# First loads in an order of their own, and the first two output tiles together, in a hybrid pooling and SSD decoder step

## The chip, the cores and the metric

The kernel runs on one core of one Trainium2 chip. The metric is device time in microseconds (us) for one execution, the median of several runs. The core has a matrix engine (TensorE, PE in the profile, with its weight loads as PEld), a vector engine (VectorE, DVE), a scalar engine (ScalarE, ACT), a general engine (GpSimd, POOL) and a sync engine (SyncE, SP) that issues nearly all the transfers. Each engine takes its instructions in one fixed order. The order of the compiled program is made beforehand by a scheduler that simulates the program, so an instruction can stand far from where the source has it.

## The reference, cut to what matters

One decoder layer works on 1024 prompt tokens and 64 sample tokens with model width 1024. All data are 32-bit floats.

```python
def swiglu(x, w_in, w_out):
    gu = x @ w_in
    g, u = gu[..., :D_FF], gu[..., D_FF:]
    return (jax.nn.silu(g) * u) @ w_out          # D_FF = 2816

def layer(x, ...):
    x = x + 0.5 * swiglu(rmsnorm(x, norm_ffn1[l]), ffn1_w_in[l], ffn1_w_out[l])
    mix, ... = token_mixing(rmsnorm(x, norm_mix[l]), ...)
    x = x + mix
    x = x + 0.5 * swiglu(rmsnorm(x, norm_ffn2[l]), ffn2_w_in[l], ffn2_w_out[l])
    return x, ...
# then one final rmsnorm
```

The token mixing (pooling branch and state-space branch with gates) is not touched by the change.

## The kernel before, in words

**Halves and splits.** The tokens are cut in two halves: half 0 has 512 columns, half 1 has 512 prompt and 64 sample columns, 576 in all, computed as two pieces of 288. Activations lie with the channel on the 128 partitions. For accuracy each operand is the sum of a high and a low part; a product of two operands is three matmuls (high by high, high by low, low by high). `load_w` loads 4 blocks of 128x128 weights (256 KB) into a `wraw` buffer (6 of them), ACT copies out the high part `wh` (L264) and DVE the low part `wl` (L265; 3 buffers each).

**Start.** `load_x` (L605 on) loads a half of x token by token in tiles of 128x512 (`xin`, L618; eight for half 0, ten for half 1), squares them on ACT (L627), finds the reciprocal root on DVE, makes diagonal matrices `dg` (L637, on DVE and POOL in turn) and multiplies by them on PE, which transposes and scales at once (`ptx`, and `pxs` for the samples). ACT, DVE and POOL then make `xn`, `hi` and `lo`. In the source the first weights come first, then x of half 0, then more weights; x of half 1 is a chain of its own. `load_consts` loads 13 small constants; `Dcol` is read from `d_skip` at every second element (L234).

**First product of an FFN.** There are 22 tiles of 128 channels (`NFF`). The first three (`N_PLAIN`) are computed directly, for half 0 and then half 1 (`ffn_in_plain`, banks `pg` and `pu`). The others use a seven-product scheme (`ffn_in`, `wino`, banks `pw`), whose operands are made from x beforehand (`combine`, much of it on POOL). The weights of a tile are combined and split for it (L405 on POOL, L411 on ACT, L412 on DVE). All but the last three tiles (`N_APART`) serve both halves with one set of weights; the last three are computed for half 0 and then, with the weights loaded again, for half 1. An `ffn_in` tile is evacuated by ACT (L504, L512) and DVE (L516 to L521), and the result `g` is stored to DRAM (`hd`, L523).

**Second product.** For each half the 22 stored tiles are loaded (`hr`, L578) and split into `hh` (ACT, L302) and `hr` (DVE, L304). Their buffers come from the `act` pool (58 buffers), of which the operands of the first product hold 56; a few come from the `fx` pool (17). Then the eight output tiles are computed one after the other over all 22 blocks (`po`), each with six weight loads, and added to x (L588). In the second FFN, `half` begins the transposes of the final output after four tiles.

**Order.** `pe` counts the PE work written so far, and side chains (`start`, `tick`) come in when it reaches their due time. `after1` starts the norm for the mixing of half 0 (`norm_split`, pace `HN_PACE`), which is needed after half 1's second product. `dma` is always SP's queue.

Of the kernel before, what the change touches and what calls it, by code (L numbers as in the profile page):

```python
# [14 lines left out]
P = 128  # L15
D = 1024
KD = D // P
# [18 lines left out]
N_ACT, N_BIG, N_PD = 58, 3, 4  # L36
N_RAW, N_W = 6, 3
N_FX, N_S, N_PDF = 17, 4, 6
N_PLAIN, N_APART = 3, 3

PRODUCTS = (("1", 0), ("2", 1), ("6", 0), ("5", 2), ("7", 0), ("3", 2), ("4", 0))

# [3 lines left out]
STEP_S = 2.5  # L46
GP = (0.7, 1.2)
PACE = 2.0
HN_PACE = 0.5
MP = 2.0  # L50
R_WAIT0 = 3.0
R_WAIT = 5.0
# [9 lines left out]
def tile_hybrid_pool_ssd_macaron(  # L62
# [23 lines left out]
    def act(shape=(P, 576), dt=F32, name="a"):  # L86
        return sp.tile(list(shape), dt, tag="act", bufs=N_ACT, name=nm(name))
# [17 lines left out]
    def fx(dt=F32, name="x"):  # L105
        if stage["name"] == "mix":
            return act((P, 576), dt, name)
        return stage["p"].tile([P, 576], dt, tag="fx", bufs=N_FX, name=nm(name))
# [111 lines left out]
    Dcol = cp.tile([P, 16], F32, tag="Dcol", name="Dcol")  # L220
    rd_n = [0]
    hp = [0]

    def load_consts():

        yield from load_cols(nr0, nr1)
        yield from load_cols(nr1, nr)
        for t, src in ((tri, c_tri), (strict, c_strict), (tri_s, c_tri_s), (strict_s, c_strict_s), (bsel, c_bsel),
                       (invcnt, c_invcnt.partition_broadcast(P)), (dtb, dt_bias[0].rearrange("(h o) -> h o", o=1)),
                       (Abc, a_log[0].partition_broadcast(P))):  # L230
            dma(t, src)
        dsk = d_skip[0].rearrange("(q h) -> h q", h=2)
        for hh in range(2):
            dma(Dcol[hh * HD : (hh + 1) * HD, :], dsk[hh].partition_broadcast(HD))  # L234
        for i in range(3):
            dma(bsel3[i * 32 : (i + 1) * 32, :], c_bsel[0:32, 0:4])
        yield 12
        for j in range(4):
            V.tensor_scalar_mul(cwh[:, j, :], cols[:, i_cw[j] : i_cw[j] + 24], 0.5)
        V.tensor_scalar_mul(cwh[:, 4, :], cols[:, i_cb : i_cb + 24], 0.5)  # L240
        S.activation(Abc, Abc, AF.Exp)
        V.tensor_scalar_mul(Abc, Abc, -1.0)
# [9 lines left out]

    ahead = {}

    def load_w(w, k0, nk, c0, ncol=P):

        if (k0, c0) in ahead:
            return ahead.pop((k0, c0))
        raw, wh, wl = (sp.tile([P, 4 * P], d, tag=t, bufs=n, name=nm(t))[:, : nk * ncol]
                       for t, d, n in (("wraw", F32, N_RAW), ("wh", F32R, N_W), ("wl", F32R, N_W)))  # L260
        dma(raw.rearrange("p (k c) -> p k c", c=ncol),
            w[k0 * P : (k0 + nk) * P, c0 : c0 + ncol].rearrange("(k p) c -> p k c", p=P))
        with tc.high_priority(hp[0]):
            S.activation(wh, raw, AF.Copy)  # L264
            V.tensor_tensor(wl, raw, wh.bitcast(F32), op=ALU.subtract)  # L265
        return wh.rearrange("p (k c) -> p k c", c=ncol), wl.rearrange("p (k c) -> p k c", c=ncol)
# [12 lines left out]
    def dense(w, rk0, nk, c0, xs, tag="pd", name="pd"):  # L279

        out = banks(xs, tag, name)
        for kb in range(0, nk, 4):
            n4 = min(4, nk - kb)
            wh, wl = load_w(w, rk0 + kb, n4, c0)
            for kk in range(n4):
                products(out, wh, wl, kk, slice(0, P), xs, kb + kk, nk)
                tick()
        return out
# [254 lines left out]
    def ffn(wi, wo, prep, after, half=None):  # L543

        X, todo, behind = [{}, {}], [], []
        for h in HALVES:
            finish(prep[h][0])
            x = prep[h][1][0]  # L550
            gen = combine(h, x[3], x[1], x[2], X[h], T_PACE)

            def first(gen):
                for p in gen:
                    if p is None:
                        return
                    yield p

            c = start(first(gen), T_AT)
            for ff in range(N_PLAIN):  # L560
                ffn_in_plain(wi, ff, x[:3])
            todo.append(c)
            behind.append(start(rest(c, gen)))
        for c in behind:
            finish(c)
        for ff in range(N_PLAIN, NFF - N_APART):
            ffn_in(wi, ff, [(h, X[h]) for h in HALVES])
        for h in HALVES:
            for ff in range(NFF - N_APART, NFF):
                ffn_in(wi, ff, [(h, X[h])])  # L570
        for h in HALVES:
            N = NTOK[h]
            parts = [], []
            for k in range(NFF):
                slot = (lambda d, n_: act((P, 576), d, n_)) if half or k < NFF - 2 else fx
                t, a = slot(F32, "hr"), slot(F32R, "hh")
                t = t[:, :N]
                dma(t, hdram[h][k])  # L578
                split(t, a[:, :N], t.bitcast(F32R))
                parts[0].append(a)  # L580
                parts[1].append(t.bitcast(F32R))
            xt = []
            for m in range(KD):
                x_ = fx(name="x")
                dma(x_[:, :N], xspill[h][m])
                po = dense(wo, 0, NFF, m * P, [(h, *parts)], name="po")[0]
                for pt, (a, b) in zip(po, PIECES[h]):
                    V.scalar_tensor_tensor(x_[:, a:b], pt[:, : b - a], 0.5, x_[:, a:b], op0=ALU.mult, op1=ALU.add)  # L588
                xt.append(x_)
                if half and m == KD // 2 - 1:  # L590
                    half(h, xt)
            after(h, xt)

# [13 lines left out]
    def load_x(h, out):  # L607
# [2 lines left out]
        N = NTOK[h]  # L610
        blocks = blocks_of(h)
        nb = len(blocks)
        raws = []
        for src, _, c in blocks:
            raws.append([])
            for q in range(2):
                t = act((P, 512), name="xin")
                dma(t[:c, :], src[:, q * 512 : (q + 1) * 512])  # L618
                raws[-1].append(t)
        yield X1_AT if h else 0.2  # L620
        ss = small((P, 4, 5), "xss", 2)
        if h == 1:
            G.memset(ss, 1.0)
        for i, (_, c0, c) in enumerate(blocks):
            for q in range(2):
                junk = act((P, 512), name="junk")
# [7 lines left out]
        dg = act((P, 576), name="dg")  # L634
        dg = [dg[:, i * P : i * P + b[2]] for i, b in enumerate(blocks)]
        for i, (_, c0, c) in enumerate(blocks):
            (V if i % 2 else G).tensor_scalar_mul(dg[i][:c, :c], ident[:c, :c], ss[:c, 2, i : i + 1])  # L637
        if h == 1:
            pq = psum("ps", "pxs")
            for k in range(KD):  # L640
# [57 lines left out]

    def after1(h, xt):
        if h == 0:  # L700
            ch["hn"] = start(norm_split([t[:, : NTOK[0]] for t in xt], 0, i_gm, hn, HN_PACE))
        for m in range(KD):
            dma(xspill[h][m], xt[m][:, : NTOK[h]])

    st = open_stage("ffn1", N_PDF)
    finish(start(load_cols(0, nr0)))
    prep1 = []
    for kb in (0, 4):
        for c0 in (0, FF):
            ahead[kb, c0] = load_w(wi1, kb, 4, c0)  # L710
        if kb == 0:
            for h in HALVES:
                o = []
                prep1.append((start(load_x(h, o)), o))
                if h == 0:
                    prep1[0][0].step()

    def turn():
        for h in HALVES:
# [759 lines left out]
```

## Time and profile before

| | us |
|---|---|
| median of 3 runs | 3026.63 (3025.07 to 3032.89) |
| the profiled execution's own time | 3030.0 |
| its span in the trace | 3028.2 |
| PE busy | 2928.0 |
| DVE busy | 1779.1 |
| ACT busy | 1279.1 |
| POOL busy | 438.1 |

Times in the rows are from the span's start. A row of the timeline has the start, the length, the engine, the line and the operation, output and input, the count, and in brackets the idle time of the engine before it with what ended it. `SPq` rows are issues of transfers, not the transfers themselves. In a row of stretches each engine's busy time stands with its number of instructions, then the granted PE clock (1.00 is full speed), the share of time in which the 16 DMA engines were busy, and GB/s. A busy PE is not PE at its peak, because matmuls overlap; the count of matmuls in a stretch tells its pace. In rows of waits the numbers are the total, the times and, in PE's waits, the longest.

### The profile page before, as it was taken

To read this page: it belongs to the slowest core of one execution; us is meant where nothing else is said; L and a number is where in the kernel's file an instruction comes from. 1 tells how busy PE (TensorE), PEld (TensorE's weight loads), DVE (VectorE), ACT (ScalarE), POOL (GpSimd) and SP (SyncE) were. 2 spreads that over 40 slices of the span, in tenths; PEclk is the share of its full clock that TensorE was granted. 3 is DMA by queue.
4 is the path that set the end of the run, shared out by engine and by line. 5 is a ranking of instruction groups with operands and counts; after the bars stand their busy time and mean duration, and the time that the engine had idled before them with its cause. 6 is when DMAs were issued, how large, how long until landed. Compare 5 with 4: busy or idle time off the path is not lost. (4 is left out here: it accounts for less than half of the span.)

```text
span 3028.2 us, 51543 instructions
## 1 busy us (share of the span) xinstructions
PE 2928.0 (97%) x19636; PEld 2714.0 (90%) x19636; DVE 1779.1 (59%) x3479; ACT 1279.1 (42%) x2580; POOL 438.1 (14%) x497
## 2 busy tenths in 40 slices
PE   6999999999999999999999999999999999999998
PEld 5999999789988878787999989999989999997898
DVE  4644347534273898777725986977775343374442
ACT  4443335423243665434424654543443333353332
POOL 3433335000000000000000110100023333350000
PEclk9999999999999999999999999999999999999999
DMA  4442224753334333445333334344443222245542
GB/s 128 132 134 92 79 83 124 225 157 119 101 96 124 113 106 96 112 121 175 97 104 103 107 112 132 93 130 133 152 133 102 72 79 75 77 144 154 170 146 72
DMA packets 527722, 356.29 MB, mean 118 GB/s; under 512 B 27418, under 2 KB 468880, under 8 KB 527466
## 3 DMA queue, kind: packets, MB, share of 16 engines
q1 hardware_dynamic: 527458, 352.99, 39.0%
q8 instruction: 154, 2.52, 0.4%
q14 instruction: 94, 0.77, 0.1%
q10 hardware_dynamic: 16, 0.00, 0.0%
HBM read 295.85 MB, written 57.29 MB: 117 GB/s over the span
## 5 line engine op out<-in xcount | busy, mean ns | idle before, releaser
L264 ACT ACTIVATE wh<-wraw 128x512 fp32r<-128x512 f32 x636 | 392.2, 619 | 853.0 <-PE po L160 287.0
L265 DVE TENSOR_TENSOR wl<-wraw,wh 128x512 fp32r<-128x512 f32 x636 | 437.4, 690 | 510.5 <-ACT wh L264 492.0
L160 PE MATMUL pw<-hi,wh 128*128 128x288 f32 (+1 forms) x1216 | 352.3, 290 | 6.4 <-DVE t L516 6.4
L160 PE MATMUL pw<-X,wh 128*128 128x256 f32 (+1 forms) x1824 | 349.7, 290 | 8.6 <-ACT t L512 7.2
L160 PE MATMUL pw<-hi,wl 128*128 128x288 f32 (+1 forms) x1216 | 351.1, 289 | 0.5 <-DVE wl L412 0.5
L160 PE MATMUL pw<-lo,wh 128*128 128x288 f32 (+1 forms) x1216 | 350.8, 289 | 0.0
L160 PEld LDWEIGHTS pw<-X,wh 128*128 128x128 f32 x1824 | 288.6, 190 | 11.1 <-ACT t L512 8.6
L160 PE MATMUL po<-hh,wh 128*128 128x288 f32 (+1 forms) x1056 | 290.8, 331 | 7.6 <-ACT hh L302 5.6
L160 PE MATMUL po<-hr,wh 128*128 128x288 f32 (+1 forms) x1056 | 290.1, 330 | 1.0 <-DVE hr L304 1.0
L160 PE MATMUL po<-hh,wl 128*128 128x288 f32 (+1 forms) x1056 | 289.4, 329 | 0.5 <-DVE wl L265 0.4
L160 PE MATMUL pw<-X,wl 128*128 128x256 f32 (+1 forms) x912 | 263.6, 289 | 0.0
L160 PEld LDWEIGHTS pw<-hi,wh 128*128 128x128 f32 x1216 | 230.6, 190 | 7.8 <-DVE t L516 7.8
L160 PEld LDWEIGHTS pw<-hi,wl 128*128 128x128 f32 x1216 | 230.4, 189 | 0.8 <-DVE wl L412 0.7
L160 PEld LDWEIGHTS pw<-lo,wh 128*128 128x128 f32 x1216 | 230.5, 190 | 0.0
L412 DVE TENSOR_TENSOR wl<-s,wh 128x512 fp32r<-128x512 f32 x176 | 129.5, 740 | 160.1 <-ACT wh L411 156.6
L160 PEld LDWEIGHTS po<-hh,wh 128*128 128x128 f32 x1056 | 180.4, 190 | 25.4 <-ACT hh L302 8.6
L160 PEld LDWEIGHTS po<-hr,wh 128*128 128x128 f32 x1056 | 180.9, 190 | 17.0 <-DVE hr L304 3.6
L160 PEld LDWEIGHTS po<-hh,wl 128*128 128x128 f32 x1056 | 180.7, 190 | 14.9 <-DVE wl L265 1.4
L411 ACT ACTIVATE wh<-s 128x512 fp32r<-128x512 f32 x176 | 110.6, 630 | 168.0 <-PE pw L160 164.6
L160 PEld LDWEIGHTS pw<-X,wl 128*128 128x128 f32 x912 | 174.0, 191 | 0.0
L160 PE MATMUL pc<-hi,wh 128*128 128x288 f32 (+1 forms) x576 | 162.1, 335 | 0.4 <-ACT craw L750 0.3
L160 PE MATMUL pc<-hi,wl 128*128 128x288 f32 (+1 forms) x576 | 159.4, 329 | 0.0
(334 smaller groups left out, 6454.3 us busy)
## 6 DMA issues: line engine op xcount, KB each, us to landing
wraw<-in_w_in_dram SPq DMA_DIRECT2D x260, 256.0 KB
wraw<-in_ffn_w_in_dram SPq DMA_DIRECT2D x224, 256.0 KB
wraw<-in_ffn_w_out_dram SPq DMA_DIRECT2D x160, 256.0 KB
ab<-acsd SPq DMA_DIRECT2D x64, 256.0 KB
wraw<-in_ssd_w_out_dram SPq DMA_DIRECT2D x64, 256.0 KB
hd<-g SPq DMA_DIRECT2D x44, 288.0 KB
hr<-hd SPq DMA_DIRECT2D x44, 288.0 KB
hd<-g SPq DMA_DIRECT2D x44, 256.0 KB
```

The lines of the kernel that those rows point to most:

```text
L160: T.matmul(out, lhsT, rhs, start=start, stop=stop, skip_group_check=free)
L264: S.activation(wh, raw, AF.Copy)
L265: V.tensor_tensor(wl, raw, wh.bitcast(F32), op=ALU.subtract)
L411: S.activation(wh, a, AF.Copy)
L412: V.tensor_tensor(wl, a, wh.bitcast(F32), op=ALU.subtract)
```

## The change

In the first loads: x of half 0 is issued first, and its squares are written ahead of all weights. The second pair of weight tiles and the ten loads of x of half 1 are held back by `hold`: a one-element copy on POOL into the buffer that is to be loaded, from a value that the first square of half 0 makes, so that the transfer must wait for it. The constants are held the same way to the first square of half 1 (but not the rows that `load_cols` loads). All of `dg` is made on DVE.

In the FFNs: only one tile of the first product is computed for each half on its own. In the second product, output tiles 0 and 1 are computed together, block by block, in each half; the x to which they are added is loaded after the products in the source. The first four `hr` and `hh` of half 0 lie in `fx`; in the first FFN the last two of half 1 still do. The norm for the mixing starts 25 us of PE work later and with a pace of 2.0 instead of 0.5.

```diff
-N_PLAIN, N_APART = 3, 3
+N_PLAIN, N_APART = 3, 1
-HN_PACE = 0.5
+HN_AT, HN_PACE = 25.0, 2.0
 ...
+    late = []
     def load_consts():
 ...
+            hold(t, late[1][:1, 0, :1])
             dma(t, src)
         dsk = d_skip[0].rearrange("(q h) -> h q", h=2)
         for hh in range(2):
+            hold(Dcol[hh * HD :], late[1][hh * HD : hh * HD + 1, 0, :1])
             dma(Dcol[hh * HD : (hh + 1) * HD, :], dsk[hh].partition_broadcast(HD))
         for i in range(3):
+            hold(bsel3[i * 32 :], late[1][i * 32 : i * 32 + 1, 0, :1])
             dma(bsel3[i * 32 : (i + 1) * 32, :], c_bsel[0:32, 0:4])
 ...
+    def hold(t, src):
+        G.tensor_copy(t[:1, :1], src)
+
-    def load_w(w, k0, nk, c0, ncol=P):
+    def load_w(w, k0, nk, c0, ncol=P, behind=None):
 ...
+        if behind is not None:
+            hold(raw, behind)
         dma(raw.rearrange("p (k c) -> p k c", c=ncol),
 ...
             for k in range(NFF):
-                slot = (lambda d, n_: act((P, 576), d, n_)) if half or k < NFF - 2 else fx
-                t, a = slot(F32, "hr"), slot(F32R, "hh")
+                own = k < 4 if h == 0 else not half and k >= NFF - 2
+                t, a = (fx(d, n_) if own else act((P, 576), d, n_) for d, n_ in ((F32, "hr"), (F32R, "hh")))
 ...
-            for m in range(KD):
-                x_ = fx(name="x")
-                dma(x_[:, :N], xspill[h][m])
-                po = dense(wo, 0, NFF, m * P, [(h, *parts)], name="po")[0]
-                for pt, (a, b) in zip(po, PIECES[h]):
-                    V.scalar_tensor_tensor(x_[:, a:b], pt[:, : b - a], 0.5, x_[:, a:b], op0=ALU.mult, op1=ALU.add)
-                xt.append(x_)
-                if half and m == KD // 2 - 1:
+            for ms in ((0, 1),) + tuple((m,) for m in range(2, KD)):
+                po = [banks([(h,)], "pd", "po")[0] for _ in ms]
+                for kb in range(0, NFF, 4):
+                    n4 = min(4, NFF - kb)
+                    for m, pts in zip(ms, po):
+                        wh, wl = load_w(wo, kb, n4, m * P)
+                        for kk in range(n4):
+                            products([pts], wh, wl, kk, slice(0, P), [(h, *parts)], kb + kk, NFF)
+                            tick()
+                for m, pts in zip(ms, po):
+                    x_ = fx(name="x")
+                    dma(x_[:, :N], xspill[h][m])
+                    for pt, (a, b) in zip(pts, PIECES[h]):
+                        V.scalar_tensor_tensor(x_[:, a:b], pt[:, : b - a], 0.5, x_[:, a:b], op0=ALU.mult, op1=ALU.add)
+                    xt.append(x_)
+                if half and ms[-1] == KD // 2 - 1:
                     half(h, xt)
 ...
         ss = small((P, 4, 5), "xss", 2)          # in load_x, now ahead of the loads
 ...
+                if h == 1:
+                    hold(t, late[0][:1, 0, :1])
                 dma(t[:c, :], src[:, q * 512 : (q + 1) * 512])
 ...
+        late.append(ss)
 ...
-            (V if i % 2 else G).tensor_scalar_mul(dg[i][:c, :c], ident[:c, :c], ss[:c, 2, i : i + 1])
+            V.tensor_scalar_mul(dg[i][:c, :c], ident[:c, :c], ss[:c, 2, i : i + 1])
 ...
-            ch["hn"] = start(norm_split([t[:, : NTOK[0]] for t in xt], 0, i_gm, hn, HN_PACE))
+            ch["hn"] = start(norm_split([t[:, : NTOK[0]] for t in xt], 0, i_gm, hn, HN_PACE), HN_AT)
 ...
-    prep1 = []
+    prep1 = [(start(load_x(h, o)), o) for h, o in ((0, []), (1, []))]
+    for _ in range(5):
+        prep1[0][0].step()
     for kb in (0, 4):
         for c0 in (0, FF):
-            ahead[kb, c0] = load_w(wi1, kb, 4, c0)
-        if kb == 0:
-            for h in HALVES:
-                o = []
-                prep1.append((start(load_x(h, o)), o))
-                if h == 0:
-                    prep1[0][0].step()
+            ahead[kb, c0] = load_w(wi1, kb, 4, c0, behind=late[0][:1, 0, :1] if kb else None)
+    prep1[1][0].step()
```

More of the change, by code (lines that the diff above doesn't have):

```diff
@@ L612, in load_x @@
         nb = len(blocks)
+        ss = small((P, 4, 5), "xss", 2)
+        if h == 1:
+            G.memset(ss, 1.0)
         raws = []
@@ L617, in load_x @@
                 t = act((P, 512), name="xin")
+                if h == 1:
+                    hold(t, late[0][:1, 0, :1])
                 dma(t[:c, :], src[:, q * 512 : (q + 1) * 512])
                 raws[-1].append(t)
+        late.append(ss)
         yield X1_AT if h else 0.2
-        ss = small((P, 4, 5), "xss", 2)
-        if h == 1:
-            G.memset(ss, 1.0)
         for i, (_, c0, c) in enumerate(blocks):
```

## The prediction

> **What bounds the kernel now.** First the page: TensorE (PE) is busy for almost the whole span, so only its holes and its slow stretches can be won.
>
> ```profile
> span 3028.2 us, 51543 instructions
> PE 2928.0 (97%) x19636; PEld 2714.0 (90%) x19636; DVE 1779.1 (59%) x3479; ACT 1279.1 (42%) x2580; POOL 438.1 (14%) x497
> ```
>
> Then the busy times in stretches of 20 us, to find the holes (columns: PE, PEld, DVE, ACT, POOL busy with counts, granted clock, DMA share, GB/s).
>
> ```profile
> 0.00:20.00 20.00, 2.95 (x13) 2.89 (x14) 4.78 (x19) 9.17 (x21) 2.15 (x10) 1.00 0.81 232
> 40.00:60.00 20.00, 12.51 (x49) 9.61 (x47) 7.67 (x26) 10.92 (x31) 2.93 (x5) 0.78 0.77 225
> 460.00:480.00 20.00, 20.00 (x164) 20.00 (x163) 10.65 (x16) 8.64 (x18) 7.74 (x8) 1.00 0.26 81
> 520.00:540.00 20.00, 16.69 (x118) 15.63 (x117) 14.37 (x21) 10.41 (x22) 7.61 (x6) 1.00 0.60 189
> 2860.00:2880.00 20.00, 16.25 (x96) 14.73 (x95) 8.19 (x12) 8.35 (x16) 0.00 (x0) 0.85 0.50 163
> ```
>
> The row at 460 is undisturbed work on two halves: 164 matmuls, PE full. At 520 there are 118, with DVE and DMA much busier: output tiles done one half at a time, beside the loads of hr. The holes are thus the start, 40 to 60, the end of each first product, and the change of half in the second. Each is in reach of the change.
>
> **First loads.** The timeline of the first 70 us, by engine:
>
> ```profile
> 1.78 4.09 SPq L618 DMA_DIRECT2D xin<-in_x_prompt_dram  x8
> 12.07 0.63 ACT L264 ACTIVATE wh<-wraw 128x512 fp32r<-128x512 f32 x1 [1.59 <-DMA wraw<-in_ffn_w_in_dram]
> 13.21 0.61 ACT L627 ACTIVATE junk<-xin 128x512 f32<-128x512 f32 x1
> 16.48 0.60 DVE L637 TENSOR_SCALAR dg<-ident,xss 128x128 f32<-128x128 f32 x2
> 17.29 4.80 PE L160 MATMUL ptx<-dg,xin 128*128 128x128 f32 x24 [14.59 <-DMA strict<-in_strict_dram]
> 18.36 1.38 SPq L234 DMA_DIRECT2D Dcol<-in_d_skip_dram  x2
> 24.71 19.85 SPq L618 DMA_DIRECT2D xin<-in_x_prompt_dram  x8
> 46.51 39.61 SPq L261 DMA_DIRECT2D wraw<-in_ffn_w_in_dram  x12
> 52.65 0.80 PE L160 MATMUL pu<-hi,wh 128*128 128x512 f32 x1 [5.79 <-ACT wh L264]
> 57.74 3.67 PE L160 MATMUL pxs<-dg,xin 64*128 64x64 f32 x16 [1.70 <-POOL dg L637]
> ```
>
> The last squares of half 0 stood on ACT behind a weight split (12.07) that waited for its own load. Then come SP's constants; while Dcol's element-wise loads drain, the DMA engines move next to nothing:
>
> ```profile
> DMA packets 2209, 0.03 MB, mean 2 GB/s; under 512 B 2209, under 2 KB 2209, under 8 KB 2209
> ```
>
> That is the window 18 to 38: 2209 tiny packets in 20 us. x half 1 is queued behind them (eight issues take 19.85), and the weights behind x half 1 (46.51), so PE stands 5.79 at 52.65 and 1.70 at 57.74. After it the granted clock (stretches of 2 us):
>
> ```profile
> 62.00:64.00 2.00, 2.00 (x9) 1.88 (x9) 0.08 (x1) 0.55 (x1) 0.00 (x0) 0.50 0.00 0
> 64.00:66.00 2.00, 2.00 (x9) 1.56 (x8) 1.51 (x2) 1.01 (x4) 0.13 (x1) 0.77 0.00 0
> ```
>
> Half speed until about 65.5. From 52.65 that is 12.9 us, less 1.7 idle: 11.2 at half speed, 5.6 lost.
>
> *The start.* Half 0 goes ahead of all weights: SP issues it 1.0 us earlier, 0.5 MB less lies ahead (2.2 us at the 232 GB/s of the first stretch), and no split stands before the last squares. The eight tiles should then land by about 10, the squares end by about 11 instead of 13.8. From there to the first ptx stays 3.5 (13.8 to 17.29): all of dg on DVE is 0.6 more for DVE, two fewer for POOL. PE starts near 14.1: **-3.2** (ends: -1.0, the issue alone; -4.5, a landing 1.3 sooner than that).
>
> The next part needs PE's pace: eight transposes, the first two-half product (pw), and the ends of neighbouring tiles of the second product, of 66 matmuls of 512 columns and of 132 of 288.
>
> ```profile
> 22.63 1.05 PE L160 MATMUL ptx<-dg,xin 128*128 128x128 f32 x8
> L160 PEld LDWEIGHTS pw<-hi,wh x16: 187/191/192, 127.1 to 133.2; 128*128 128x128 f32 x16
> 641.37 0.69 DVE L588 SCALAR_TENSOR_TENSOR x<-po,x 128x512 f32<-128x512 f32 x1 [0.23 <-PE po L160]
> 656.33 0.69 DVE L588 SCALAR_TENSOR_TENSOR x<-po,x 128x512 f32<-128x512 f32 x1 [0.23 <-PE po L160]
> 801.04 0.82 DVE L588 SCALAR_TENSOR_TENSOR x<-po,x 128x288 f32<-128x288 f32 x2 [0.38 <-PE po L160]
> 818.64 0.82 DVE L588 SCALAR_TENSOR_TENSOR x<-po,x 128x288 f32<-128x288 f32 x2 [0.38 <-PE po L160]
> ```
>
> A tile of half 0 takes 14.96, of half 1 17.60: 0.227 and 0.133 a matmul.
>
> *x half 1 ahead of the constants.* It is held to the first square of half 0, when SP has only just issued the first weights, so the hold costs nothing; it should land by about 21 instead of 50. What can go: 5.79 + 1.70 + 5.6 = 13.1. What is late next is the weights behind the constants, for Dcol's 20 us do not vanish; they move. In that time PE lives on weight tiles already loaded: six in wraw and three split, 9 tiles, at a quarter of 48 matmuls each. A tile lasts 12 x 0.227 = 2.7 and nine last 24.5, more than 20. With only half of them loaded (12) the stall would be 8, plus 5.6 of half clock, which eats the 13.1. From PE's start to the first two-half product the trace has 127.1 - 17.3 = 109.8; its work is 144 x 0.227 + 288 x 0.133 + 128 transposes of 0.131 + 1.8 = 89.6, so 20.2 is lost there in all. I take **-11**, nearer to the upper value because half 1's transposes, 10 us of PE work, now fall inside Dcol's shadow and stretch the weights; ends +1 and -20.
>
> *The holds*: 2 + 10 + 13 one-element copies on POOL. The nearest row is POOL's memset of xss:
>
> ```profile
> 1.35 0.11 POOL L623 MEMSET xss<- 128x20 f32 x1
> ```
>
> So 25 x 0.11 = 2.8 on POOL. The first twelve fall into the first 20 us, where POOL was busy for 2.15; the thirteen for constants stand ahead of combine work not needed before 127: 0 (at worst they delay half 0's lo splits by 13 x 0.11 = 1.4). Whatever is behind a held DMA on SP waits with it; ACT's exponent of Abc waits for a held load, so ACT could stand there. That is in the +1 end.
>
> **The products.** In the first FFN the stores of g mark each tile of the first product; the additions into x, of which two pairs stand above, the end of each tile of the second:
>
> ```profile
> 450.68 1.97 SPq L523 DMA_DIRECT2D hd<-g  x2
> 471.84 1.97 SPq L523 DMA_DIRECT2D hd<-g  x2
> 506.35 0.34 SPq L523 DMA_DIRECT2D hd<-g  x1
> 549.88 0.32 SPq L523 DMA_DIRECT2D hd<-g  x1
> 671.65 0.69 DVE L588 SCALAR_TENSOR_TENSOR x<-po,x 128x512 f32<-128x512 f32 x1
> 2659.28 1.96 SPq L523 DMA_DIRECT2D hd<-g  x2
> 2734.83 0.34 SPq L523 DMA_DIRECT2D hd<-g  x1
> 2858.00 0.68 DVE L588 SCALAR_TENSOR_TENSOR x<-po,x 128x512 f32<-128x512 f32 x1
> 3011.65 0.82 DVE L588 SCALAR_TENSOR_TENSOR x<-po,x 128x288 f32<-128x288 f32 x2 [7.26 <-PE po L160]
> ```
>
> A paired tile takes 21.16 (450.68 to 471.84). Six single ones, 3 per half, are the same matmuls as three paired: 63.5 (9.95 and 11.2 each, by columns). They took 549.88 + 0.32 - 473.81 = 76.4 in FFN 1 and, from 2661.24 to 2735.17, 73.9 in FFN 2: 12.9 and 10.4 lost, most of it in half 1. Why: hr loads come between, and ACT, which takes its work in order, stands on them (the view of tile hr, 490 to 563):
>
> ```profile
> L578 SPq DMA_DIRECT2D hr<-hd x23: 339/433/1603, 496.4 to 562.5; - x23
>   ACT hh L302: 24.1, 13
> ```
>
> 13 times, 24.1 us; PE's next product waits for a copy (L512) behind it.
>
> *One single tile per half instead of three.* Matmuls unchanged. Two tiles of weights per FFN are loaded and split once less (2 x 1 MB; 14 ACT and 14 DVE splits, 8 POOL sums): beside PE, 0 by itself. The loss falls on 2 tiles instead of 6, but the same hr loads press into less time. A third of 12.9 and 10.4 would be about 4; I take 5.5 left per FFN: **-7.4** and **-4.9** (ends: all left, 0; none left, -12.9 and -10.4).
>
> *First two output tiles together.* Half 0's product after the stores took 671.65 - 549.88 = 121.8 against 8 x 14.96 = 119.7; in FFN 2 123.2: 2.1 and 3.5 lost. The cover of the loads shrinks, since 40 us of single tiles are gone; in return the first sweep over 22 blocks lasts 29.9, and four blocks get fx buffers that don't wait for the first product. I take **0** and **-1**. Half 1: 818.64 - 671.65 = 147.0 against 8 x 17.60 = 140.8, and 153.7 in FFN 2, of which some 4.5 are the 36 transposes of final outputs: 6.2 and 8.4 lost, behind late hr. With a first sweep of 35 us and four (FFN 1) or eight (FFN 2) act buffers more free for preloads: **-4.2** and **-5.4** (ends 0, and all of it). PSUM: two or four of six pd banks at the start, enough. The loads of the old x now stand behind the products in the source, but have a whole sweep to land: 0. The norm chain of half 0, now 25 later and slower, takes some 60 of half 1's 147: hidden.
>
> Sum: -3.2 - 11 - 7.4 - 4.9 - 0 - 1 - 4.2 - 5.4 = -37.1. The profiled execution took 3030.0 (span 3028.2), 3.4 above the median 3026.6; against its own time this gives **2993** (2990 against the median, a difference too small to measure).
>
> **The clock, weighed.** FFN 2's change of half has no long hole, yet (PE's waits from 2860 to 2884: us in total, times, longest; and a stretch):
>
> ```profile
> PE po L160 <- ACT hh L302: 2.8, 2, 1.8
> 2876.00:2878.00 2.00, 1.76 (x8) 1.41 (x7) 0.53 (x1) 1.19 (x3) 0.00 (x0) 0.50 0.00 0
> ```
>
> Two gaps, the longer 1.8, were enough for half speed. The Trainium skill, "TensorE: Matmul & The Clock Gate", Part 1, has the clock fall after an idle window of about 3.4 us; taken as one unbroken hole, this trace does not agree. By that rule short remaining stalls would cost no clock, and the sum would be some 3 us lower per FFN; I go by the row.
>
> **The rivals.**
> (a) The hr loads are not hidden. Now 22 go in 66 us, 3.1 each. After the change 17 loads follow the first buffer release; the last block is wanted about 6 + 14 + 21 x 1.36 = 49 later. At 3.1 plus 2.7 for landing and split the last is there at 55: 6.4 of stall and about 3 of clock per FFN, 2993 + 19 = **3012**. For it: 12 are loaded only beside the second product now. Against: the pace is set by buffer releases of six slow tiles, not by DMA (81 to 189 GB/s in the rows).
> (b) All that is named goes, but for a few us per place: both ends of the first loads, and four fifths of the products' 43.5: 3030 - 4.5 - 20 - 34.8 = **2971**.
> (c) Nothing in sum: Dcol's shadow lands on half-loaded weights (+1), the single tiles' whole loss stays on the two left, and of the rest only FFN 2's half change gains: 3030 - 3.2 + 1 - 5.4 = **3022**.
> (d) Slower: SP, in order, puts each hr behind a wo load that waits for its split (wraw waits for wl there), at 4.5 per load. The last block comes at 17 x 4.5 + 2.7 = 79, a stall of 30 per FFN, against gains of 37: 3030 - 37 + 60 = **3053**. It decides from 2.7 + 17p = 49 + 18.5, p = 3.8. For it: the twelve weight loads at 46.51 went out one in 3.3, each behind a free buffer. Against: the hr loads' own 3.1, with single tiles beside them.
>
> **How the numbers follow.** Forecast (2980 to 3004) 0.50; (a) 0.20; (b) 0.11; (c) 0.09; (d) 0.10. About 0.3% (9 us) is what a measurement can tell from no change; (c) lies mostly inside it. Faster 0.82, same 0.08, slower 0.10. From 2966, just below (b), to 3018, above (a), about 0.8.
>
> **What would show it.** First ptx near 14 and not 17; x half 1 issued before Dcol; no PE wait above 3 us and no half clock between 40 and 70; first pw near 113. Single tiles: one store per half, at about 10.5 and 14 us after the last pair. At half changes PE at 75 matmuls per 10 us without a dip of the clock. Wrong: ACT or SP standing on a held constant; PE waiting for hh in the first sweep with hr's DMA behind it.

## The result, and the profile after

The changed kernel takes 2995.8 us (median of 4 runs, 2994.1 to 2997.8), against 3025.9 for the kernel before beside it (4 runs, 3022.8 to 3032.9). The ratio is 0.9898, 95% interval 0.9879 to 0.9916. The profiled execution took 2994.1, its span is 2992.3: 35.9 less than the span before. By the medians it is 30.1 less; the profile of before lies 4.2 above its median and that of after 1.7 below, so a reading by stages shows some 6 us that the medians don't have.

First two rows of the page: against before, PE is busy 17 us less and idle 19 us less.

```profile
span 2992.3 us, 51430 instructions
PE 2911.1 (97%) x19636; PEld 2699.1 (90%) x19636; DVE 1746.3 (58%) x3456; ACT 1264.2 (42%) x2552; POOL 409.6 (14%) x501
```

Next the start, from the timeline (start, duration, engine, line, operation):

```profile
0.74 0.46 SPq L271 DMA_DIRECT2D wraw<-in_ffn_w_in_dram  x1
11.10 4.88 SPq L642 DMA_DIRECT2D xin<-in_x_prompt_dram  x8
11.13 0.63 ACT L649 ACTIVATE junk<-xin 128x512 f32<-128x512 f32 x1
11.96 0.17 DVE L652 TENSOR_TENSOR xss<-xss 128x4 f32<-128x4 f32 x1 [6.75 <-ACT junk L649]
12.70 0.69 DVE L275 TENSOR_TENSOR wl<-wraw,wh 128x512 fp32r<-128x512 f32 x1
13.67 0.69 DVE L275 TENSOR_TENSOR wl<-wraw,wh 128x512 fp32r<-128x512 f32 x1 [0.27 <-ACT wh L274]
16.05 0.87 DVE L659 TENSOR_SCALAR dg<-ident,xss 128x128 f32<-128x128 f32 x4
16.39 2.93 PE L160 MATMUL ptx<-dg,xin 128*128 128x128 f32 x12 [13.87 <-DVE dg L659]
46.20 1.37 SPq L237 DMA_DIRECT2D Dcol<-in_d_skip_dram  x2
```

The last square ends at 11.8, two us earlier than before, but the first transpose comes only 0.9 earlier. The chain of small DVE steps between them began at 11.96 and was cut open by two weight splits (12.70, 13.67), so dg came at 16.05. One weight tile still went out ahead of x (0.74). x half 1 went out at 11.10, before Dcol, which now comes at 46.20. The view of the DMA engines from 46 to 67 shows that Dcol's shadow moved and did not vanish; the busy times from 40 to 60, and of the whole stage from 17 to 128 in the kernel before and then in this one, show what it cost. Behind them stand the weight loads of the first two-half product (`pw`) and, from PE's timeline, its longest wait:

```profile
DMA packets 2616, 0.14 MB, mean 7 GB/s; under 512 B 2412, under 2 KB 2615, under 8 KB 2615
```

```profile
40.00:60.00 20.00, 19.84 (x115) 16.50 (x114) 15.48 (x37) 8.60 (x21) 10.68 (x19) 1.00 0.21 50
```

```profile
17.00:128.00 111.00, 99.19 (x597) 88.70 (x598) 68.88 (x126) 51.23 (x118) 49.62 (x49) 0.94 0.36 104
```

```profile
17.00:128.00 111.00, 104.28 (x671) 94.42 (x671) 74.48 (x135) 53.70 (x127) 53.75 (x60) 1.00 0.41 118
```

```profile
L160 PEld LDWEIGHTS pw<-hi,wh x16: 187/191/192, 117.8 to 123.8; 128*128 128x128 f32 x16
```

```profile
84.97 0.53 PE L160 MATMUL pu<-hi,wl 128*128 128x288 f32 x2 [2.87 <-DVE wl L275]
```

From 40 to 60 PE is full at clock 1.00, where before it had 12.51 of 20 at 0.78. Over the stage it is busy 5 us more (99.19 before, 104.28 now), with a mean clock of 1.00 instead of 0.94; the first two-half product comes at 117.8 and not 127.1. The longest wait left is 2.87, on a split.

Then the products: the stores of g, and the additions that end each half of the second product.

```profile
504.82 1.97 SPq L533 DMA_DIRECT2D hd<-g  x2
530.32 0.34 SPq L533 DMA_DIRECT2D hd<-g  x1
657.84 0.69 DVE L607 SCALAR_TENSOR_TENSOR x<-po,x 128x512 f32<-128x512 f32 x1
798.45 0.82 DVE L607 SCALAR_TENSOR_TENSOR x<-po,x 128x288 f32<-128x288 f32 x2 [0.37 <-PE po L160]
2676.54 1.97 SPq L533 DMA_DIRECT2D hd<-g  x2
2702.01 0.34 SPq L533 DMA_DIRECT2D hd<-g  x1
2830.74 0.68 DVE L607 SCALAR_TENSOR_TENSOR x<-po,x 128x512 f32<-128x512 f32 x1
2975.36 0.82 DVE L607 SCALAR_TENSOR_TENSOR x<-po,x 128x288 f32<-128x288 f32 x2 [7.26 <-PE po L160]
```

The two single tiles take 530.66 - 506.79 = 23.9 in both FFNs, against 21.2 of work: 2.7 lost. Half 0's second product takes 657.84 - 530.32 = 127.5 and 128.7 (before 121.8 and 123.2): here time was given back. Half 1 takes 140.6 and 144.6, its pure work. A sweep is one pass over the 22 stored blocks. The next two rows are a stretch in the first sweep of half 0 and one across the half change. Behind them stand PE's waits for `hh` from 526 to 572, and, from the groups of 490 to 600, the loads of hr and what waited for them:

```profile
550.00:560.00 10.00, 8.93 (x36) 6.32 (x35) 3.80 (x6) 3.58 (x7) 0.00 (x0) 1.00 0.87 290
660.00:670.00 10.00, 10.00 (x77) 10.00 (x76) 4.17 (x6) 3.47 (x6) 0.00 (x0) 1.00 0.68 216
```

```profile
PE po L160 <- ACT hh L312: 3.0, 4, 1.2
```

```profile
L589 SPq DMA_DIRECT2D hr<-hd x33: 319/440/1532, 509.1 to 599.1; - x33
```

```profile
  ACT hh L312: 26.4, 20
```

In the sweep 36 matmuls pass in 10 us where 45 are normal, and ACT stands 20 times on a load of hr. At the half change 77 pass and the clock stays at 1.00.

Where the 35.9 went, stage by stage, from the rows above and their counterparts before:

| stage | predicted | measured |
|---|---|---|
| start of PE | -3.2 | -0.9 |
| from there to the first pw | -11 | -8.4 |
| first product, FFN 1 / FFN 2 | -7.4 / -4.9 | -10.3 / -7.7 |
| second product, half 0 | 0 / -1 | +5.7 / +5.6 |
| second product, half 1 | -4.2 / -5.4 | -6.4 / -9.0 |
| mixing and the start of FFN 2 | 0 | -4.9 |
| end | 0 | +0.4 |

### The profile page after: what moved, and what is told of

It reads as the page before. It is cut to its first block, busy times and chain, and to the rows that moved or that the text cites. A ratio compares the mean times of both kernels' runs of the same rounds, so it can differ in the third digit from the quotient of the medians.

```text
span 2992.3 us, 51430 instructions
## 1 busy us (share of the span) xinstructions
PE 2911.1 (97%) x19636; PEld 2699.1 (90%) x19636; DVE 1746.3 (58%) x3456; ACT 1264.2 (42%) x2552; POOL 409.6 (14%) x501
## 5 line engine op out<-in xcount | busy, mean ns | idle before, releaser
L274 ACT ACTIVATE wh<-wraw 128x512 fp32r<-128x512 f32 (+1 forms) x636 | 391.3, 618 | 803.6 <-PE po L160 239.0
L275 DVE TENSOR_TENSOR wl<-wraw,wh 128x512 fp32r<-128x512 f32 (+1 forms) x636 | 437.5, 689 | 461.7 <-ACT wh L274 439.6
L160 PE MATMUL pw<-X,wh 128*128 128x288 f32 (+1 forms) x1824 | 347.3, 289 | 0.4 <-ACT t L522 0.4
L160 PE MATMUL pw<-X,wl 128*128 128x288 f32 (+1 forms) x912 | 263.0, 288 | 0.0
L422 DVE TENSOR_TENSOR wl<-s,wh 128x512 fp32r<-128x512 f32 x160 | 114.1, 714 | 176.2 <-ACT wh L421 173.4
L421 ACT ACTIVATE wh<-s 128x512 fp32r<-128x512 f32 x160 | 101.1, 632 | 181.3 <-PE pw L160 179.0
```

What stands on the lines that cost most here:

```text
L160: T.matmul(out, lhsT, rhs, start=start, stop=stop, skip_group_check=free)
L421: S.activation(wh, a, AF.Copy)
L422: V.tensor_tensor(wl, a, wh.bitcast(F32), op=ALU.subtract)
```

## The experiments

**The two halves of the change by themselves.** `e1_first_loads` is the changed kernel with the products, slots and norm chain of before; `e2_products` is the kernel before with those of the change.

```diff
 e1_first_loads
-N_PLAIN, N_APART = 3, 1
+N_PLAIN, N_APART = 3, 3
...
+                slot = (lambda d, n_: act((P, 576), d, n_)) if half or k < NFF - 2 else fx
...
+                po = dense(wo, 0, NFF, m * P, [(h, *parts)], name="po")[0]
```

> Only the first loads changed (order, holds, all of dg on DVE); the products as in the kernel before. Theory (the first loads and the products add up): the first two-half product starts near 118 us instead of 127, and the whole run is 9 to 12 us shorter than before, about 3015. Rival (the start's gain is real but is given back because the products then wait for the same weights): first pw near 118, but the time within 3 us of before.

> Only the products changed (one single tile per half, first two output tiles together, four hr blocks in fx, later norm chain); the first loads as in the kernel before. Theory (both parts add up): first pw at 127, FFN 1 about 11 and FFN 2 about 11 shorter, the run 22 to 27 us shorter than before, about 3001. Rival (part of the products' gain comes from the earlier start shifting the schedule): less than 15 us shorter.

Measured: 3023.0 (0.9973, 0.9961 to 0.9985) and 3010.1 (0.9938, 0.9925 to 0.9950), some 8 and 19 us below before. Together 27, and the whole change 31 by its ratio; the difference lies inside the intervals. The first loads are worth about a quarter of the gain (8.2 of 31), the products about three fifths (18.8), and the 4 that are left can't be told from nothing. Both came out below what was expected, 9 to 12 and 22 to 27.

**Is the shadow Dcol's own?** `e5_dcol_before` is the kernel before, but `d_skip` comes in one contiguous broadcast, and two POOL copies cut Dcol out of it. SP's order stays otherwise.

```diff
-        dsk = d_skip[0].rearrange("(q h) -> h q", h=2)
-        for hh in range(2):
-            dma(Dcol[hh * HD : (hh + 1) * HD, :], dsk[hh].partition_broadcast(HD))
+        dma(dskb, d_skip[0].partition_broadcast(P))
```

> The kernel before, in which only the load of Dcol is another: d_skip comes as 32 contiguous elements for each partition, and two POOL copies pick every second one. The order of all other transfers is the same. Theory (the 20 us without data after 18 are Dcol's element-wise loads): the DMA engines go on moving data after 20 us, x half 1 is issued without the 7 us stops, the 5.8 us wait of PE at 52 and the half clock vanish, first pw 9 to 15 us earlier than before's 127, the run about 10 us shorter. Rival (the stop is the copy of state_pool or bsel's loads, which are unchanged): first pw within 3 us of 127.

Measured: 3023.4 (0.9978, 0.9967 to 0.9990). The DMA engines from 18 to 38, x half 1 on SP, the first pw, and PE's wait for the first weight split in this run:

```profile
DMA packets 1985, 2.65 MB, mean 132 GB/s; under 512 B 824, under 2 KB 824, under 8 KB 1976
```

```profile
21.39 3.72 SPq L620 DMA_DIRECT2D xin<-in_x_prompt_dram  x8
```

```profile
L160 PEld LDWEIGHTS pw<-hi,wh x16: 187/191/192, 120.2 to 126.2; 128*128 128x128 f32 x16
```

```profile
PE pu L160 <- ACT wh L266: 2.5, 1, 2.5
```

In the same 20 us 2.65 MB moved, not 0.03; the eight issues of x half 1 took 3.72, not 19.85; the wait of 5.79 became 2.5; and the first pw came 6.9 earlier, less than the 9 to 15 expected. The shadow is that of the element-wise load. By the ratio the whole run is 6.7 shorter: one load of another form brings most of what the first part of the change brings (8.2 in e1).

**Where half 0's sweep loses.** Five kernels, each the changed kernel with one edit. `e3_three_apart` has three single tiles per half again. `e4_one_by_one` has the second product's tiles one by one in the source.

```diff
 e3_three_apart
-N_PLAIN, N_APART = 3, 1
+N_PLAIN, N_APART = 3, 3
 e4_one_by_one
-            for ms in ((0, 1),) + tuple((m,) for m in range(2, KD)):
+            for ms in tuple((m,) for m in range(KD)):
```

> The changed kernel with three single tiles per half again; the first two output tiles still together. Theory (single tiles cost by themselves, but cover the hr loads): the single tiles lose 10 and 8 us again, the first sweep of half 0 loses about 2 instead of 7.5, so the run is 7 to 10 us slower than the changed kernel, about 3004. Rival (the 5 us that half 0's second product lost come from computing two tiles together, not from the missing cover): 16 to 20 us slower, about 3014.

> The changed kernel with the output tiles of the second product computed one after the other again (loads of the old x still behind the products in the source); one single tile per half. Theory (with the cover gone the first sweep is too short for the hr loads, and half 1's first sweep again waits for its last blocks): half 0's second product loses 12 to 18 us instead of 7.5, half 1's 4 to 8 instead of 0 to 1, the run 15 to 35 us slower than the changed kernel, about 3020. Rival (the freed act buffers and the later norm chain made half 1's change smooth, and the scheduler already interleaves two tiles by itself): within 6 us of the changed kernel.

Measured: 3005.9 (0.9923, 0.9910 to 0.9937) and 3016.0 (0.9955, 0.9943 to 0.9968). With three single tiles half 0's second product takes 121.8 and 123.7 again, what it took before, while the single tiles lose their 11 again: the short run of single tiles pushes the lateness of hr into the sweep. Of the 10.3 and 7.7 won in the first product, the sweep gives 5.7 and 5.6 back. Without the pair half 0 takes 136.2 and 132.3, so the pair saves 8.7 and 3.5 there. It is the source order that e4 undoes: in its compiled order the first two tiles still overlap, and their additions end 40.4 and 45.2 behind the last store in FFN 1 (38.2 and 40.0 in the changed kernel).

`e9_x_later` holds the loads of the old x behind the last hr of the half; `e12_hr_pool` gives the loads of hr to POOL's queue, past SP's order; `e10_fx_last` gives the fx buffers to the last four blocks of half 0 and not the first.

```diff
 e9_x_later
+                    hold(x_, last)
                     dma(x_[:, :N], xspill[h][m])
 e12_hr_pool
-                dma(t, hdram[h][k])
+                G.dma_start(t, hdram[h][k])
 e10_fx_last
-                own = k < 4 if h == 0 else not half and k >= NFF - 2
+                own = k >= NFF - 4 if h == 0 else not half and k >= NFF - 2
```

> The changed kernel in which the loads of the old x of the second product (8 x 256 KB a half) are held behind the split of the half's last hr block. Theory (in the first sweep of half 0 those 2 MB compete with hr and the weights; at about 280 GB/s they take 7.5 us): half 0's second product loses 2 to 5 us instead of 7.5 and 8.7, the run 6 to 12 us shorter than the changed kernel. Rival (the sweep waits for the order of the blocks or for the splits on ACT, not for bandwidth): within 3 us.

> The changed kernel with all hr loads issued by POOL instead of SP. Theory (half 0's first sweep is paced by a loop: SP issues an hr only behind a weight load that waits for a free buffer, which waits for DVE's split, behind ACT's, which stands behind the split of an hr not yet landed): with hr out of SP's order half 0's second product loses 2 to 4 us instead of 7.5 and 8.7, the run 6 to 12 us shorter than the changed kernel. Rival (act buffers coming free, or ACT standing on hr loads from whatever queue, set the pace): within 3 us of the changed kernel, or slower by up to 5 if POOL's issues are slow.

> The changed kernel with the last four instead of the first four hr blocks of half 0 in fx. Theory (fx buffers come free later than the first act buffers, so blocks 0 to 3 arrived after blocks 4 to 10 and the sweep began late): half 0's second product loses 2 to 5 us instead of 7.5 and 8.7, half 1 unchanged, the run 5 to 11 us shorter than the changed kernel. Rival (bandwidth sets the sweep, whatever the order): within 3 us.

Measured: 2999.0 (0.9895, 0.9881 to 0.9909), 3000.4 (0.9901, 0.9886 to 0.9916) and 3009.2 (0.9933, 0.9920 to 0.9947). Half 0's second product takes 127.8 and 127.7 in e9, 126.3 and 128.0 in e12, 132.6 and 133.0 in e10. The traffic of the old x doesn't set its pace: without it the half is within about 1 us of the changed kernel. The total of e12 lies as near, but there a gain and a new loss cancel. In the changed kernel the last twelve loads of hr (530.71 to 557.9) stand between weight loads on SP, and these wait until the split has freed a weight buffer. SP's waits from 526 to 566:

```profile
SPq L271 <- DVE wl L275: 16.1, 6, 4.9
```

In e12 the last hr of half 0 is issued at 542.5, and from 545 on the sweep runs at full pace. The same 20 us, in the changed kernel and in e12:

```profile
545.00:565.00 20.00, 18.21 (x73) 12.91 (x72) 8.91 (x15) 7.56 (x13) 0.00 (x0) 1.00 0.65 212
545.00:565.00 20.00, 20.00 (x90) 16.46 (x88) 8.18 (x13) 7.57 (x14) 5.37 (x10) 1.00 1.06 355
```

That is 17 matmuls more, worth 3.8 at 45 in 10 us (in FFN 2, 71 against 86). But e12 had lost time before: on POOL the issues of hr stood behind a step of g until 532.46, one wait of PE was 4.03, and from 540 to 545 the clock was 0.66. So 45 matmuls passed from 530 to 545, against 54 in the changed kernel:

```profile
540.00 0.73 PE L160 MATMUL po<-hh,wh 128*128 128x512 f32 x2 [4.03 <-ACT hh L312]
```

So SP's order does set the pace of the later part of the sweep; e12 only moved the loss to its beginning. The slots matter as well. In e10 the blocks with act buffers are wanted four blocks earlier, 4 x 1.36 = 5.4, and the half lost 5.1 and 4.3 more. The agreement is in part chance: in FFN 1 some 10.2 us ran at half clock, as this row of e10 shows, and half of that is 5.1 by itself; in FFN 2 the clock didn't fall.

```profile
552.00:562.00 10.00, 8.58 (x19) 5.14 (x18) 3.48 (x6) 3.65 (x6) 0.00 (x0) 0.51 0.60 202
```

If the blocks arrive too late for the sweep, a longer sweep must hide it. `e13_three` takes three tiles together in half 0, loads Dcol contiguously, and gives two of the first weight splits to POOL, out of the way of DVE's chain.

```diff
+for ms in (((0, 1, 2),) + ... if h == 0 else ((0, 1),) + ...):
+        dma(dskb, d_skip[0].partition_broadcast(P))
+            (eng or V).tensor_tensor(wl, raw, wh.bitcast(F32), op=ALU.subtract)
```

> The changed kernel with three edits that act in different stages: Dcol from contiguous loads, the low parts of two first weight tiles on POOL instead of DVE, and three output tiles together in half 0's second product (two in half 1). Theory: the first transposes 1.0 to 1.4 us earlier (the newton steps no longer stand behind two splits on DVE); first pw 2 to 5 us earlier than 117.8; half 0's second product loses 2 to 4 us instead of 7.5 and 8.7, since a sweep of three lasts 45 us; the run 12 to 18 us shorter than the changed kernel, about 2981. Rival (the loop of weights and hr only gets longer with three tiles, for each hr then waits behind more weight loads): half 0's second product loses as much as now or more, the run only 3 to 6 us shorter.

Measured: 2986.4 (0.9855, 0.9839 to 0.9872), the fastest version here: its interval lies below the changed kernel's, its median 9 us lower (13 by the ratios). Half 0's second product, and the start:

```profile
532.04 0.34 SPq L535 DMA_DIRECT2D hd<-g  x1
653.96 0.68 DVE L609 SCALAR_TENSOR_TENSOR x<-po,x 128x512 f32<-128x512 f32 x1
12.82 2.48 POOL L277 TENSOR_TENSOR wl<-wraw,wh 128x512 fp32r<-128x512 f32 x2 [5.62 <-ACT wh L276]
12.90 1.20 DVE L328 TENSOR_TENSOR xss<-xss 128x4 f32<-128x4 f32 x1
14.14 1.19 DVE L329 SCALAR_TENSOR_TENSOR xss<-xss 128x4 f32<-128x4 f32 x1
15.55 0.16 DVE L328 TENSOR_TENSOR xss<-xss 128x4 f32<-128x4 f32 x1
```

Half 0 takes 121.9, and 123.2 in FFN 2: 5.6 less in each, and the half behind it doesn't get longer (140.3 and 144.6). At the start nothing was won: while POOL split, DVE's two steps of four elements a partition took 1.20 and 1.19 instead of 0.16, PE began at 16.9, and the first pw came at 118.9.

**What made half 1 run through.** The changed kernel's half 1 loses nothing, the kernel before 6.2 and 8.4. In question were the pair, the slots, and where the old x is loaded. `e8_old_slots` has the slot rule of before; `e11_x_first` loads the old x ahead of the products again; `e14_old_loop` has the whole old loop, with the new slots.

```diff
 e8_old_slots
-                own = k < 4 if h == 0 else not half and k >= NFF - 2
+                slot = (lambda d, n_: act((P, 576), d, n_)) if half or k < NFF - 2 else fx
 e11_x_first
+                    xs_.append(fx(name="x"))
+                    dma(xs_[-1][:, :N], xspill[h][m])
                 po = [banks([(h,)], "pd", "po")[0] for _ in ms]
 e14_old_loop
-            for ms in ((0, 1),) + tuple((m,) for m in range(2, KD)):
+            for m in range(KD):
+                x_ = fx(name="x")
+                dma(x_[:, :N], xspill[h][m])
+                po = dense(wo, 0, NFF, m * P, [(h, *parts)], name="po")[0]
```

> The changed kernel with the old rule for the buffers of hr and hh (half 0 all in act but for the last two blocks in the first FFN). Theory (the eight act buffers left free for half 1's preloads made its half change smooth): half 1's second product again loses 4 to 8 us in each FFN, while half 0's first sweep loses 2 to 4 less than 7.5 and 8.7, because its first blocks are loaded in their natural order; together 4 to 10 us slower than the changed kernel. Rival (the pair of tiles alone makes half 1 smooth, and the fx blocks, loaded after blocks 4 to 8, only delay half 0): 4 to 8 us faster than the changed kernel.

> The changed kernel with the loads of the old x written ahead of the products again, as before; two tiles still together. Theory (half 1's change became smooth because the loads of the old x no longer go ahead of hr and the first weights; neither two tiles together nor the fx blocks did it): half 1's second product again loses 4 to 8 us in each FFN, the run 8 to 16 us slower than the changed kernel. Rival (it is the later norm chain in FFN 1 and the whole of the new loop in FFN 2): half 1 stays within 2 us of 140.8 (and 4.5 more in FFN 2), the run within 3 us of the changed kernel.

> The changed kernel with the loop of the second product written as before: eight tiles one by one, each with its load of the old x and its buffer ahead of the tile's weights. Single tiles (one per half), slot rule, late norm chain and first loads stay. It asks what made half 1's second product run through. Theory, the loop: the pair, or the x load behind the products, each takes the gap away alone (one run with the pair but x ahead, and one without the pair but x behind, both ran through), so with neither the gap is back: half 1 loses 4 to 8 in FFN 1 and 5 to 9 in FFN 2 (takes 145 to 149 and 150 to 154), the clock dips at the half change, and the time is about 3022 (e4's 3016 and 6 or more). Rival, the rest: the single tiles, slots or the late chain made it, or half 0's own delay gives the loads of half 1 their lead: half 1 loses under 2.5 in both FFNs, time about 3016. Half 0 should lose 12 to 17 either way, since without the pair its last blocks are wanted as early as in e4.

Measured: 3015.4 (0.9946, 0.9931 to 0.9962), 3000.5 (0.9906, 0.9891 to 0.9921) and 3015.2 (0.9947, 0.9929 to 0.9965). With e11 half 1 still runs through (141.4 and 144.6): the place of x is not it. What half 1's second product lost, against 140.8 of work in FFN 1 and 145.3 in FFN 2:

| | tiles one by one | first two together |
|---|---|---|
| old slots | before 6.2 / 8.4; e1 6.7 / 6.2 | e8 0.5 / 1.3 |
| new slots | e4 1.3 / 1.7; e14 1.0 / 1.3 | after 0 / 0; e3 0 / 0 |

Either of the two is enough to within 0.5 to 1.7, which is why no run that undid one of them brought the gap back; both theories that I had set against each other for e4, e8 and e14 were too simple. The cell at the upper left isn't clean, though: before and e1 also have three single tiles and the old norm chain, and no run has the old slots and the old loop with the rest of the change. In FFN 1 the old chain stands in the way itself. In before, seven of its squares run on ACT behind the split of the last block, the next weight split comes only at 694.35, and PE waits for it, its longest wait in that half, and runs at a clock of 0.60 and less from 696 to 700:

```profile
690.71 3.74 ACT L329 ACTIVATE sq<-x 128x512 f32<-128x512 f32 x7
695.02 0.53 PE L160 MATMUL po<-hh,wh 128*128 128x288 f32 x2 [1.51 <-ACT wh L264]
```

So a part of the 6.2 may be the chain's, which the change starts later; that wasn't tried by itself. The last hr issue of half 1 in FFN 1 shows what differs. One row each from before, e8, e14 and after:

```profile
686.37 0.50 SPq L578 DMA_DIRECT2D hr<-hd  x1
```

```profile
683.89 0.50 SPq L588 DMA_DIRECT2D hr<-hd  x1
```

```profile
675.50 0.42 SPq L589 DMA_DIRECT2D hr<-hd  x1
```

```profile
669.24 0.42 SPq L589 DMA_DIRECT2D hr<-hd  x1
```

Half 0 ends (its last addition begins) at 671.65, 668.36, 664.08 and 657.84. Counted from there, that issue ends at 15.2 and 16.0 with the old slots, at 11.8 and 11.8 with the new. Landing and split took 3.1 to 3.8 more: the block's split on ACT ends at 18.6, 19.5, 15.0 and 15.6. The block is wanted after 21 blocks of 0.80 where one tile runs, 16.8, and after 33.6 where two do. Of these four only the kernel before is late, by 1.8. This reading is one of FFN 1 alone. In FFN 2 the last issue ends 32.9, 34.3, 21.6 and 25.1 behind half 0, and the compiled order of the old loop runs the first two tiles nearly together (their additions come 40.5 and 46.3 behind half 0 in before, 32.5 and 40.2 in e14). There e8, with the latest issue, loses 1.3 and before 8.4; why stays open.

In half 0, e8 shows what the slots are worth there, beside e10: without the first four blocks in fx, half 0 takes 136.9 and 132.0, 9.4 and 3.3 more than in the changed kernel. Up to 5.1 of the 9.4 is half clock (0.50 for 10.2 us between 550 and 565). In e4 and e14 (134.8 and 133.9) half 0 is longer too.

## Why the prediction was right, and where it was not

The forecast of 2993 holds within 3 us, and its likeliest case happened. In part that is luck. The steps miss by up to 6.6 on both sides, and the mixing, which the change doesn't touch, gave 4.9 of the 35.9 between the two profiles; without it they show 31.0, where 37.1 was added up from the profile of before. By the medians the gain was 30.1.

- **The start, -3.2, measured -0.9.** The step that failed is "from there to the first ptx stays 3.5": the squares did end two us earlier, but the stretch grew to 4.6, because DVE's order put two weight splits into it. e13 took them out and shows that the step has no cheap cure on POOL. One weight tile went ahead of x all the same.
- **x half 1 ahead of the constants, -11, measured -8.4.** As argued: no wait over 3 us and no half clock between 40 and 70. Dcol's 20 us moved (46 to 67) and were covered by the loaded weights. The first pw came at 117.8 and not 113. (The prediction's working lets the half clock of before last until about 65.5; by its own rows that is 64.9, and the term 5.3 instead of 5.6.) What is late next is a split: DVE is busy for 19.40 of the 20 us from 60 to 80, and PE's 2.87 waits on it. A part of that busy time is waiting beside POOL: one and the same step of DVE took 1.06 while POOL worked and 0.45 once POOL's last step had ended at 84.0. The stretch, and the two steps:

```profile
60.00:80.00 20.00, 17.97 (x106) 15.28 (x105) 19.40 (x27) 13.10 (x30) 15.80 (x16) 1.00 0.45 129
81.32 1.06 DVE L483 TENSOR_TENSOR X<-xn,X 128x288 fp32r<-128x288 f32 x1
84.84 0.45 DVE L483 TENSOR_TENSOR X<-xn,X 128x288 fp32r<-128x288 f32 x1
```

- **The holds, 0.** The sign that I had named as wrong showed once: SP stood for 6.5 (from 33.4 to 40.0) on the first held constant. The hold's copy was not late because of work on POOL: it waited for a step of half 1's norm on DVE (L325), and not for the first square on ACT, which began at 30.36. The wait on SP, and the first copy:

```profile
SPq L233 <- POOL tri L261: 6.5, 1, 6.5
39.40 0.57 POOL L261 COPY tri<-xss 1x1 f32<-1x1 f32 x1 [3.19 <-DVE xss L325]
```

  The long times of L240 that follow are no waits for holds, whose copies were all done by 43.0. They are Dcol's shadow: an issue of 8.74 behind it, where the kernel before, which has no holds, has 13.08 for three loads of x behind its own. SP's timeline, after and before:

```profile
52.21 8.74 SPq L240 DMA_DIRECT2D bsel<-in_bsel_dram  x1
24.71 13.08 SPq L618 DMA_DIRECT2D xin<-in_x_prompt_dram  x3
```

  PE was full from 40 to 60. What the 6.5 cost further on wasn't tried.
- **Single tiles, -7.4 and -4.9, measured -10.3 and -7.7.** "5.5 left per FFN" was 2.7, in both.
- **First two tiles, half 0: 0 and -1, measured +5.7 and +5.6.** This is the step that failed most. It put at nothing the cover that the loads lose with 40 us of single tiles gone, because a first sweep of 29.9 and four blocks in fx buffers "that don't wait for the first product" would make up for it. They didn't. Those four loads went out in places 6, 8, 10 and 11 of 22, behind act-buffered blocks of which one had gone at 164.8 and the next at 509; and from 530 to 558 the last twelve loads shared SP's order with weight loads that waited 16.1 in all for a buffer. The sign named for it, PE waiting for hh in the first sweep, showed. Rival (a) had nearly the size (6.4 of stall in each FFN; the sweep's whole loss was 7.8 and 9.0), but not SP's part in it, and it let the single tiles' gain stand at the forecast's size. Rival (d) had SP's order, at a price far too high. That the loss is one of late arrival is shown by e13, SP's part by e12, and e8 and e10 show that the slots helped all the same. For landing and split the runs have 3.1 to 3.8, not 2.7.
- **Half 1: -4.2 and -5.4, measured -6.4 and -9.0.** Of the two reasons given, the first sweep of 35 us and the act buffers freed, each leaves at most 1.7 of the loss when the other is undone (e8, e4, e14). But none of these runs has the old norm chain, which stood in the way on ACT in FFN 1, and none shows what removed the loss in FFN 2. How much of the gain here is the two reasons' own stays open in part.
- **The clock.** The prediction went by the row in which a gap of 1.8 gave 0.50. In the changed kernel four waits of at most 1.2 left it at 1.00; in e14's sweep, with 3.0 the longest, it fell to 0.50 again (534 to 538). The longest wait doesn't decide alone, though: this stretch of e8 has one of 2.87 and stays at 1.00. What decides stays open.

```profile
2746.00:2756.00 10.00, 6.63 (x27) 4.41 (x26) 3.05 (x5) 2.83 (x5) 0.00 (x0) 1.00 0.41 121
```

- **Mixing, 0, measured -4.9.** The change doesn't touch it. From the first product of the mixing to FFN 2 it took 1421.1 before, 1415.0 after, and 1415.8 to 1424.0 in the twelve experiments, with and without parts of the change. This is about the 6 us by which the two profiles differ more than the medians. Most of it can be seen: before ran 10.2 us of the mixing at half clock (the longest such stretch is this row), after 3.4, which is 3.4 us of the 6.1, and PE idled 2.6 more. Why two executions differ in that stays open.

```profile
2194.90:2201.60 6.70, 6.70 (x30) 6.70 (x30) 3.26 (x15) 0.63 (x1) 0.00 (x0) 0.50 0.34 109
```

## What to carry to other kernels

A transfer that is late is late in the next place too: when a stretch that covers loads is shortened, add up by when the last load is wanted after the change (blocks times pace), and by when its buffer comes free, and compare the two for every place, as for half 1 above. Take the order in which loads really go out from the trace; don't take it from the pool's name. When an edit leaves the total where it was, look at the stretches: a gain and a new loss can cancel, as in e12. When undoing either of two edits changes nothing, undo both before you call either idle; no run here did that with the rest of the change in place.

## What the runs showed of the hardware

- An element-wise load of 2 x 1024 numbers held the queue behind it for some 20 us, wherever it stood (18 to 38 before, 46 to 67 after), at 2 to 7 GB/s; contiguous, the shadow is gone (e5).
- DVE steps of 0.16 took 1.20 and 1.19 while POOL split weights (e13): each ended when one of POOL's two splits of 1.24 did. The Trainium skill, "SBUF — State Buffer", section "Who interferes with whom", says that a DVE instruction with two inputs in SBUF and a GpSimd instruction that reads SBUF exclude each other, and that the later one waits for the whole of the other. These rows agree, and so do those of the changed kernel's start, 1.06 beside POOL and 0.45 after it.
